# Who waits for the last store: the final semaphore wait of a row-mean kernel moved from SyncE to TensorE

## Chip, cores and metric

The kernel runs on one core of a Trainium2 chip. The time is device microseconds of that core; for the kernel before, three runs were taken and the median is given. Beside it there is one execution taken by the hardware profiler, with the records of its instructions, its semaphores and its DMA packets. The engines are called PE (TensorE), DVE (VectorE), ACT (ScalarE), POOL (GpSimd) and SP (SyncE), as in the profile.

## The reference

The input `x` is 32 x 512 x 1024 in float32 (67.1 MB). Each row of 1024 numbers is summed and divided by 1024:

```python
def reference(x, divisor):
    return (np.sum(x, axis=-1) / divisor).astype(np.float32)   # 32 x 512
```

## The kernel before

The 16384 rows are spread over the 128 partitions, 128 rows for each: 15 "first" rows, 97 "main" rows and 16 "last" rows per partition. SP issues every load and every store. Eight bulk loads (2 rows, then five of 16 rows, then two of 15 rows) go in turn through three large buffers, each with a semaphore of its own (`in_bulk0` to `in_bulk2`, numbers 99 to 101); a load waits until DVE, and ACT where it took rows, has finished with the buffer (lines L143 and L144). DVE sums whole rows with `reduce_sum` (L215). ACT takes a few rows of the last two bulk loads with an accumulating activation (L183). POOL scales the sums that are finished early (L157, L161). The last 16 rows of a partition come in four pieces of falling size; DVE's `both_halves` (L205) and ACT sum these into `fin`, already scaled. The order on each engine is written out by hand. PE computes nothing: its instructions are its share of the barriers among the engines at the start (recorded at L261 and L119), in which POOL raises semaphore 97 and the four others wake on it.

Three stores bring the result out, all issued by SP: `res0` at L148 (semaphore `out_first`, number 104), `res` at L150 (`out_main`, 105), and `fin` at L238, which waits until `done` (109) has reached 2 and adds 16 to `landed` (110) when it has landed. After that SP has three more steps. At L240 it waits for the first two stores (the second of these waits is carried by the instruction of L243), at L243 it clears the range of the kernel's other semaphores (99 to 109), and at L244 it waits until `landed` is 16 and takes 16 off again. `landed` is allocated after the others and lies outside the cleared range, so that the clearing need not wait for the last store.

Of the kernel before, what the change touches and what calls it, by code (L numbers as in the profile page):

```python
# [35 lines left out]
def kernel(  # L36
# [6 lines left out]
    nc = tc.nc  # L43
# [55 lines left out]
    landed = nc.alloc_semaphore("landed")  # L99
# [141 lines left out]
    ids = [s.num for s in sems.values()]  # L241
    assert max(ids) - min(ids) + 1 == len(ids)
    nc.sync.sem_clear(range(min(ids), max(ids) + 1))  # L243
    nc.sync.wait_ge(landed, 16).then_inc(landed, -16)  # L244


# [33 lines left out]
```

## Time and profile before

| what | value |
|---|---|
| median of 3 runs | 160.44 us (160.24 to 160.52) |
| span of the profiled execution, first to last instruction of the program | 159.3 us |
| DVE busy | 116.7 us (73%) |
| ACT busy | 18.6 us (12%) |
| POOL busy | 1.0 us (1%) |
| PE | no busy time; its last instruction is in the barrier at 1.8 us |
| DMA queue, share of 16 engines | 98.1%, 67.18 MB |
| last store (`fin`, 8.0 KB): issue, and issue to landing | 157.85 us, 1.4 us |

The span runs from the program's first instruction, the issue of the first load, to the end of its last, the wait of L244. What the device does before the first and after the last instruction of the program is in the time but not in the span; the two differ by 1.1 us here. The results give no time for the profiled execution itself, so its span is set beside the median of the three runs. The page counts waits, branches and DMA issues as no busy time; they are found as single records with a start and a duration in nanoseconds, in the answers for a source line. In those answers PE's sequencer stands as PEldq, SP's as SPq, and so on.

### The profile page before, as it was taken

Reading aid. Unit: us, or ns where it says so; the run is one execution under the profiler, and the core shown is the slowest. Engines: PE = TensorE matmul, PEld = TensorE weight load, DVE = VectorE, ACT = ScalarE, POOL = GpSimd, SP = SyncE. Lnnn points to the kernel's source line nnn. Section 1 sums busy time; section 2 is a strip of 40 time slices with the busy share of each in tenths; the row PEclk is TensorE's granted clock in tenths of the full one; section 3 lists DMA queues with packets and bytes.
Section 4 is the critical chain, followed back from the end, with each engine's and each line's share of the span. In section 5 each row is a group of like instructions: output and inputs, shape, how many; then the busy total and the mean of one; then the engine's idle time right before and its main releaser. Section 6 shows DMA issues by size and latency. Waiting matters only on the chain.

```text
span 159.3 us, 144 instructions
## 1 busy us (share of the span) xinstructions
DVE 116.7 (73%) x32; ACT 18.6 (12%) x35; POOL 1.0 (1%) x7
## 2 busy tenths in 40 slices
DVE  0500009999499994999949999499989990399296
ACT  3000000000000000000000000000009100392196
POOL 0000000000000000000000000000000001000000
DMA  8996996996996997979969969969996999889894
GB/s 296 494 527 263 527 527 263 527 527 263 527 527 263 527 444 346 527 313 477 527 263 527 527 263 527 494 278 463 494 494 262 478 494 494 350 350 525 344 401 154
DMA packets 2160, 67.18 MB, mean 422 GB/s; under 512 B 624, under 2 KB 752, under 8 KB 880
## 3 DMA queue, kind: packets, MB, share of 16 engines
q1 hardware_dynamic: 2160, 67.18, 98.1%
HBM read 67.11 MB, written 0.07 MB: 422 GB/s over the span
## 4 chain that ended last, share of the span: by engine, by line
DMA 67%; DVE 30%; another core or an unknown queue 1%; issue 0%
DMA bulk<-in_x_dram 67%; DVE res L215 29%; DVE bulk L205 1%; DVE tail L205 0%; DVE pb L205 0%; DVE fin L205 0%
## 5 line engine op out<-in xcount | busy, mean ns | idle before, releaser
L215 DVE TENSOR_REDUCE res<-bulk 128x16 f32<-128x16384 f32 (+3 forms) x8 | 110.0, 13754 | 37.7 <-DMA bulk<-in_x_dram 37.7
L183 ACT ACTIVATE junk<-bulk 128x1024 f32<-128x1024 f32 (+1 forms) x16 | 15.6, 973 | 137.2 <-DMA bulk<-in_x_dram 137.2
L205 DVE CUSTOM_DVE_ANT_0 bulk<-bulk 128x512 f32<-128x512 f32 (+1 forms) x9 | 5.5, 665 | 3.1 <-DMA bulk<-in_x_dram 3.1
L183 ACT ACTIVATION_READ_ACCUMULATOR junk<-bulk 128x1 f32 x16 | 3.0, 187 | 0.0
L183 ACT ACT_TABLE_LOAD x1 | 1.3, 1283 | 1.9 <-PEq L119 1.9
L157 POOL TENSOR_SCALAR res<-res 128x97 f32<-128x97 f32 x1 | 0.5, 465 | 129.8 <-DVE res L215 129.8
L205 DVE DVE_READ_ACCUMULATOR2_ANT fin<- 128x1 f32 x10 | 0.8, 82 | 0.0
L183 ACT ACTIVATE junk<-tail 128x737 f32<-128x737 f32 x1 | 0.8, 789 | 0.0
L205 DVE CUSTOM_DVE_ANT_0 bulk<-bulk,part 128x192 f32<-128x192 f32 x1 | 0.4, 420 | 0.3 <-DMA bulk<-in_x_dram 0.3
L205 DVE CUSTOM_DVE_ANT_0 tail<-tail 128x304 f32<-128x304 f32 x1 | 0.5, 476 | 0.0
L205 DVE CUSTOM_DVE_ANT_0 pb<-pb 128x209 f32<-128x209 f32 x1 | 0.4, 379 | 0.1
L161 POOL TENSOR_SCALAR res<-res 128x15 f32<-128x15 f32 x1 | 0.3, 262 | 15.6 <-DVE res L215 15.6
L183 ACT ACTIVATION_READ_ACCUMULATOR junk<-tail 128x1 f32 x1 | 0.2, 187 | 0.0
L153 POOL MEMSET pb<- 128x2 f32 x1 | 0.1, 99 | 1.5 <-POOLq L119 1.5
L261 POOL MEMSET const-bfloat16-1.0<- 128x1 bf16 x1 | 0.1, 101 | 0.0
L261 POOL MEMSET const-uint8-127<- 128x1 uint8 x1 | 0.1, 101 | 0.0
L261 POOL MEMSET const-float32-0.0<- 128x1 f32 x1 | 0.1, 98 | 0.2 <-issue 0.2
L261 POOL MEMSET const-float32-1.0<- 128x1 f32 x1 | 0.1, 98 | 0.0
L205 DVE DVE_READ_ACCUMULATOR2_ANT pb<- 128x1 f32 x1 | 0.1, 84 | 0.0
L205 DVE DVE_READ_ACCUMULATOR2_ANT part<- 128x1 f32 x1 | 0.1, 83 | 0.0
## 6 DMA issues: line engine op xcount, KB each, us to landing
bulk<-in_x_dram SPq DMA_DIRECT2D x2, 7680.0 KB, 39.3
bulk<-in_x_dram SPq DMA_DIRECT2D x1, 5440.0 KB, 32.0
bulk<-in_x_dram SPq DMA_DIRECT2D x1, 1872.0 KB, 23.5
bulk<-in_x_dram SPq DMA_DIRECT2D x1, 1024.0 KB, 4.6
tail<-in_x_dram SPq DMA_DIRECT2D x1, 672.0 KB, 24.7
pb<-in_x_dram SPq DMA_DIRECT2D x1, 208.0 KB, 24.8
bulk<-in_x_dram SPq DMA_DIRECT2D x5, 40.8
out_dram<-res SPq DMA_DIRECT2D x1, 48.5 KB, 1.6
```

Of the source, the lines that this page charges most:

```text
L153: nc.gpsimd.memset(pb[:, D - c15 :], 0.0).then_inc(pool)
L157: nc.gpsimd.tensor_scalar_mul(out=res, in0=res, scalar1=scale).then_inc(pool)
L161: nc.gpsimd.tensor_scalar_mul(out=res0, in0=res0, scalar1=scale).then_inc(pool)
L183: nc.scalar.activation(scratch, src, COPY, scale=by, accum_out=dst).then_inc(count)
L205: return nc.vector.tensor_tensor_reduce(out=src[:, :h], in0=src[:, :h], in1=src[:, h:], scale=by, scalar=ahead, op0=ADD, op1=ADD, accum_ou ...
L215: nc.vector.reduce_sum(out=dst[:, :m], in_=rows, axis=AX).then_inc(dve)
L261: nc = _bacc.Bacc("TRN2", target_bir_lowering=False, num_devices=1)
```

## The change

One line, the last of the kernel's body. The wait on `landed`, with the subtraction that goes with it, is issued on PE's queue where it was on SP's. In the built program the two kernels differ in the engine of this one instruction and in nothing else: all other instructions, their order on each engine, their semaphores and their waits are the same. SP's last instruction is then the clearing of L243; PE's last is the wait of L244, right behind its part of the starting barrier.

```diff
     ids = [s.num for s in sems.values()]
     assert max(ids) - min(ids) + 1 == len(ids)
     nc.sync.sem_clear(range(min(ids), max(ids) + 1))
-    nc.sync.wait_ge(landed, 16).then_inc(landed, -16)
+    nc.tensor.wait_ge(landed, 16).then_inc(landed, -16)
```

## The prediction

> **What bounds the kernel now.** I read the page first, for the engines and the chain; then the DMA answer for the last store; then the records of the two lines at which PE and SP do the same kind of step; last the semaphore records of the trace after the program's end.
>
> ```profile
> span 159.3 us, 144 instructions
> DVE 116.7 (73%) x32; ACT 18.6 (12%) x35; POOL 1.0 (1%) x7
> ...
> DMA 67%; DVE 30%; another core or an unknown queue 1%; issue 0%
> ```
>
> The span is loading and DVE's row sums. The change touches neither: no load, sum or store moves, so everything up to the landing of the last store stays where it is. PE has no busy time at all, so nothing of its own is delayed by a wait.
>
> ```profile
> out_dram<-fin SPq DMA_DIRECT2D x1, 8.0 KB, 1.4
> ```
>
> ```profile
> L244 SPq EVENT_SEMAPHORE  x1: 17/17/17, 159.3 to 159.3; - x1
> ```
>
> The last store is issued at 157.85 us and takes 1.4 us; its sixteenth increment is recorded at 159.259. SP's wait begins to execute at 159.275, 16 ns later, takes 17 ns, and the span ends at 159.292. This is the only instruction that changes its engine. What the same instruction costs on PE stands in the starting barrier, where all engines wake on one increment of POOL's:
>
> ```profile
> L119 SPq EVENT_SEMAPHORE  x2: 17/17/17, 1.5 to 1.8; - x2
> L119 ACTq EVENT_SEMAPHORE  x2: 17/17/17, 1.5 to 1.8; - x2
> L119 DVEq EVENT_SEMAPHORE  x2: 21/21/21, 1.5 to 1.8; - x2
> L119 PEldq EVENT_SEMAPHORE  x2: 51/51/51, 1.5 to 1.8; - x2
> ```
>
> PE's takes 51 ns where SP's takes 17. In the records, POOL's increments are at 1.159, 1.487 and 1.814; SP starts 16 ns after each, PE 28 or 29 ns after.
>
> So inside the span little can happen. The time, however, is 160.44 us and the span 159.29: 1.15 us lie around it. The semaphore records go on after the span, and there a semaphore that no line of the kernel touches, number 2, is raised in two runs of nine steps, with a sweep over nearly all other semaphore numbers between them. Times in us from the start of the span, as the records have them:
>
> ```
> semaphore 2, first pass:   2.129  157.924 157.963 158.007 159.437 159.480 159.518 159.553 159.599
> sweep, numbers 207..255 from 159.562, 156..206 from 159.632, 54..104 from 159.667,
>        105..155 from 159.670, 7..53 from 159.815 to 160.164
> semaphore 2, second pass: 160.388 160.423 160.461 160.504 160.528 160.626 160.664 160.698 160.745
> ```
>
> I read this as a check-in of the five engines in a fixed order, out (five records) and back (four). The first record is at 2.129, when only PE has ended its program (its last instruction ended at 1.894; ACT, DVE, POOL and SP had work to come): PE is first. The next comes 119 ns after ACT's last instruction ended at 157.805, and two more follow at 39 and 44 ns: ACT, POOL and DVE had finished. Then nothing until 159.437, 145 ns after SP's last instruction: SP is fifth, the turning point. Four steps back, at 159.599, the pass is over. The last sweep (7 to 53) begins only after that fourth step, it ends last, and the second pass begins 224 ns behind it: this is PE's. A third pass of nine, from -0.373 to -0.002, ends just before the first instruction and has the same steps.
>
> That order makes SP the cheapest engine to be late: four check-ins are already made while it waits, and only four steps (162 ns) follow it. PE is the dearest: the other four queue behind it, and the whole pass is still to run.
>
> **The change, part by part.** All from the landing at 159.259, which is common.
>
> 1. *Taken from SP.* 16 ns to wake, 17 ns to execute, 145 ns from there to SP's check-in (159.292 to 159.437), and 162 ns of return to the end of the pass: 340 ns. SP's last instruction is now the clearing of L243, recorded at 158.462 for 45 ns, so SP is ready some 0.75 us before the landing, and takes its place in the pass without delay.
>
> 2. *Given to PE: the wait.* 29 ns to wake and 51 ns to execute: 80 ns where SP had 33, so 47 ns more. The span shows this alone: 159.34 instead of 159.29. Bounds: SP's own 33 ns (no difference) and 80.
>
> 3. *Queued behind it on PE: its check-in.* Nothing else of the program stands behind PE's wait, but its check-in does, and ACT, POOL, DVE and SP wait in line for that. Before, it was over at 2.129, hidden behind 157 us. PE's step from the end of the same kind of instruction to its check-in is 1.894 to 2.129, 235 ns. Bounds: SP's 145 and PE's 235. I take 235: same engine and same step, and PE's gap from the end of its sweep to the second pass (224 ns) is as long. That is 90 ns more than SP's.
>
> 4. *The pass.* With PE late it runs whole. All four others are then waiting, as in the second pass, whose nine records take 357 ns (160.388 to 160.745); the one before the program took 371. Instead of 162, that is 195 ns more; 209 at the other bound.
>
> Sum: 80 + 235 + 357 = 672 ns after the landing instead of 340, so +0.332 us to the end of the first pass. PE's sweep starts behind the end of the pass as before and takes as long, so the rest moves by the same amount: 160.44 + 0.33 = 160.77. It is set against the median of three runs, because no separate time of the profiled execution is given; the trace supports that the closing is in the time, since from the span's end to the second pass is 1.10 us (159.292 to 160.388), against the 1.15 between span and median. Below, with SP's prices for points 2 and 3, the pass alone remains: +0.195. Above, with 371 for the pass: +0.346.
>
> [...]
>
> **The rivals.** The line at which a change counts is 0.2% of 160.44, 0.32 us, about what a measurement of this kernel can tell from no change. My sum lies just above it.
>
> *A: the full pass behind PE, as above.* 160.77, with its bounds 160.64 to 160.79 and the scatter of the runs (0.2 below and 0.08 above the median) around it.
>
> *B: the closing is not in the time.* If the time ends with the program's last instruction and the 1.15 us lie elsewhere (before the first instruction, say), point 2 alone remains: +0.047, 160.49. For it: the results do not say where the time ends. Against it: the closing fits the 1.15 us so closely.
>
> *C: PE is no slower than SP in these steps.* The 51 ns and 235 ns might belong to the program's start, when loads are being started beside them. Then PE's steps cost 33 and 145, and +0.195 is left: 160.64. Against it: PE is the slow one at the other end too, with 216 ns from the end of the pass to its sweep where SP's takes 125 (159.437 to 159.562). [...]
>
> *D, the other side: not slower.* The pass is not a fixed order but goes on from whoever is last. If the other four can check in while PE still waits and PE then turns at once into its sweep, PE no longer sits through the 162 ns of SP's return: it would pass at 159.259 + 80 + 235 = 159.574 instead of 159.599, a gain of 0.025 us, and at SP's prices 159.437, a gain of 0.162: 160.28 to 160.42. It decides if the records of number 2 show four check-ins before the landing. Against it: the pass before the program and the second one behind it have the same steps in the same order, and ACT, POOL and DVE checked in one after another within 83 ns though POOL had been idle since 148.2 us.
>
> *E: the change does not do what it says.* The build differs in the engine of that one instruction, and a wait for 16 on a semaphore that only the last store raises can't pass early; so 160.44, at little chance.
>
> **How the numbers follow.** A 0.74, B 0.09, C 0.07, D 0.08, E 0.02. Within A the nearest rows put the time above the line, and costs that I can't see from a PE that never waited this late add rather than subtract; I give 0.61 of its 0.74 to slower and 0.13 to within 0.2%. B, C and E are within. D by its own price is within; with a median of 160.24 it would read as faster, so half of it goes there. Slower 0.61, within 0.13 + 0.09 + 0.07 + 0.04 + 0.02 = 0.35, faster 0.04. The range goes from just below B, 160.45, to 161.00, A's upper bound of 160.79 with some 0.2 of scatter; D and E and the tail of A stay outside. A's own range is 160.64 to 161.00.
>
> **What would show it right or wrong.** In the profile of the changed kernel: L244 stands under PEldq, about 51 ns long and some 29 ns behind the last landing; the span is 0.05 us longer and all before it is unchanged. Semaphore 2 has no record near 2.1 us and none between there and the landing; nine records follow PE's end by 235 ns and take about 357; the sweep of 7 to 53 is 0.33 us later, counted from the landing. Four check-ins of number 2 ahead of the landing would show D; PE steps of 17 and 145 ns would show C; a closing that moves by 0.33 us with a time that does not would show B. A span that differs elsewhere by more than 0.1 us would mean that I have overlooked an effect before the landing.

## The result and the profile after

The changed kernel takes 160.74 us (median of 12 runs, 160.62 to 161.10) against 160.42 us (12 runs, 160.24 to 160.79) of the kernel before. The ratio is 1.0021, 95% interval 1.0014 to 1.0028: slower by 0.22 to 0.45 us.

The page of the changed kernel, in the lines that answer to those shown of before, hides this. Its span is even shorter:

```profile
span 159.0 us, 144 instructions
DVE 116.7 (73%) x32; ACT 18.7 (12%) x35; POOL 1.0 (1%) x7
...
DMA 67%; DVE 31%; another core or an unknown queue 1%; issue 0%
```

Where the two spans part can be found in the chain that ended last. It is the same, piece by piece and to 0.05 us, but for one stretch of loading (columns: start and length in us, what). Of the kernel before:

```profile
79.89 39.92 DMA bulk<-in_x_dram
119.81 0.02 issue
119.83 11.90 DVE res L215
```

Of the kernel after:

```profile
79.88 39.51 DMA bulk<-in_x_dram
119.39 0.02 issue
119.41 11.90 DVE res L215
```

The loads of that stretch, which the change doesn't touch, were 0.41 us quicker in this execution. The last store therefore landed at 158.900 us where it landed at 159.259. In the runs below, which have the same loads, the landing lies anywhere from 158.99 to 159.26. So the span of a single execution can't show an effect of this size; what follows the landing can. First, the answers for L244 and for the starting barrier:

```profile
L244 PEldq EVENT_SEMAPHORE  x1: 51/51/51, 158.9 to 158.9; - x1
```

```profile
L119 SPq EVENT_SEMAPHORE  x2: 17/17/17, 1.5 to 1.8; - x2
...
L119 PEldq EVENT_SEMAPHORE  x2: 51/51/51, 1.5 to 1.9; - x2
```

The wait now stands with PE's sequencer and takes the 51 ns of PE's other waits. The store itself landed as quickly as before:

```profile
out_dram<-fin SPq DMA_DIRECT2D x1, 8.0 KB, 1.4
```

Then the semaphore records behind the program, in us, of the changed kernel:

```
semaphore 2, first pass:  159.258 159.293 159.331 159.375 159.398 159.496 159.535 159.569 159.616
sweep 7..53:              159.833 to 160.180
semaphore 2, second pass: 160.404 160.438 160.477 160.521 160.544 160.643 160.681 160.715 160.762
```

No check-in comes near 2.1 us any more, and none before the landing. All nine follow PE's wait, with the steps that the second pass has, to 1 ns. From the landing, in ns ("wake" is the time from the store's last increment to the start of the wait's own record):

| | before (SP) | after (PE) | forecast for PE |
|---|---|---|---|
| wake | 16 | 28 | 29 |
| execute the wait | 17 | 51 | 51 |
| end of the wait to the check-in | 145 | 279 | 235 |
| from there to the end of the first pass | 162 | 358 | 357 |
| landing to end of first pass | 340 | 716 | 672 |
| landing to end of second pass | 1486 | 1862 | 1818 |

By these records the closing, from the landing to the end of the first pass, is 0.376 us longer. Of this, 0.196 us are the pass (358 ns instead of 162): four more steps on the way out take 140 ns, and the way back is 56 ns longer, because its first step, behind the fifth check-in, takes 98 ns where it took 43. The other 0.180 us are PE's own steps (12 ns more to wake, 34 to execute, 134 to check in). The time of this profiled execution is 160.64 us, 0.12 us less than the moment of its last check-in, 160.762.

### The profile page after: what moved, and what is told of

Same layout as the page of the kernel before. It is cut to its first block, busy times and chain, and to the rows that moved or that the text cites. A ratio compares the mean times of both kernels' runs of the same rounds, so it can differ in the third digit from the quotient of the medians.

```text
span 159.0 us, 144 instructions
## 1 busy us (share of the span) xinstructions
DVE 116.7 (73%) x32; ACT 18.7 (12%) x35; POOL 1.0 (1%) x7
## 4 chain that ended last, share of the span: by engine, by line
DMA 67%; DVE 31%; another core or an unknown queue 1%; issue 0%
DMA bulk<-in_x_dram 67%; DVE res L215 29%; DVE bulk L205 1%; DVE pb L205 0%; DVE tail L205 0%; DVE fin L205 0%
```

## The experiments

All edits are against the kernel before; the diffs show the lines that matter and leave out where an added semaphore is allocated. "Closing" is the stretch from the last store's landing to the ninth check-in of the first pass; it is 340 ns before and 716 ns after the change.

**The wait on ScalarE**

```diff
-    nc.sync.wait_ge(landed, 16).then_inc(landed, -16)
+    nc.scalar.wait_ge(landed, 16).then_inc(landed, -16)
```

Expected:

> The wait for the last store on ScalarE, otherwise the kernel before. Theory (a fixed order PE, ACT, POOL, DVE, SP and back; whoever waits holds up all behind it): ACT wakes in about 20 ns, executes in 17, checks in 119 (ACT's row of before) to 145 ns (SP's) later, and then eight steps less the first one are left: 358 - 35 = 323 ns. From the landing to the end of the first pass 480 to 505 ns against 340 before: 0.14 to 0.17 us slower than before, 0.2 us faster than with PE. In the semaphore records one check-in (PE's) near 2.1 us, the other eight behind the landing. Rival (it is PE that is slow, the order is nothing): ACT executes in 17 ns as SP does, so within 0.05 us of before, with three or four check-ins ahead of the landing.

Measured: ratio 1.0009 (1.0001 to 1.0018), that is 0.02 to 0.29 us slower. In its answer for L244:

```profile
L244 ACTq EVENT_SEMAPHORE  x1: 17/17/17, 159.0 to 159.0; - x1
```

ACT's wait costs the 17 ns that SP's costs, and yet the kernel is slower. One check-in, at 2.128, is ahead of the landing (159.016), eight are behind it, from 159.204 to 159.526. Wake 21, execute 17, check-in 150 and rest of the pass 322 ns make a closing of 510 ns, 0.17 us more than before. The order of the pass costs time: the rest of the pass is 322 ns here and 162 with SP, and ACT's own steps account for 10 ns of the difference.

**The wait on GpSimd**

```diff
-    nc.sync.wait_ge(landed, 16).then_inc(landed, -16)
+    nc.gpsimd.wait_ge(landed, 16).then_inc(landed, -16)
```

Expected:

> The wait for the last store on GpSimd, otherwise the kernel before. Theory of the fixed order: PE and ACT have checked in before the landing, seven records follow it. POOL wakes in 16 to 21 ns, executes in 17, checks in some 145 ns later, and 358 - 73 = 285 ns of the pass are left: about 465 ns against 340, 0.12 us slower than before. Rival (PE alone is slow): within 0.05 us of before.

Measured: ratio 1.0035 (1.0021 to 1.0048), 0.34 to 0.77 us slower, the dearest of all. The expectation, 0.12 us, was wrong in size. Two check-ins (2.146 and 157.720) are ahead of the landing and seven behind, and the pass still needs 285 ns, both as the order says. But POOL's step from the wait to its check-in is 562 ns, not 145:

```profile
L244 POOLq EVENT_SEMAPHORE  x1: 17/17/17, 159.2 to 159.2; - x1
```

The wait ends at 159.168, POOL's check-in stands at 159.730. The closing is 887 ns, 0.55 us more than before, which the time bears out.

**The wait on VectorE**

```diff
-    nc.sync.wait_ge(landed, 16).then_inc(landed, -16)
+    nc.vector.wait_ge(landed, 16).then_inc(landed, -16)
```

Expected:

> The wait for the last store on VectorE, otherwise the kernel before. Theory of the fixed order: PE, ACT and POOL have checked in before the landing, six records follow it. DVE wakes in 28 ns, executes in 21, checks in 145 to 184 ns later, and 358 - 117 = 241 ns of the pass are left: 435 to 475 ns against 340, 0.10 to 0.13 us slower than before. Rival (PE alone is slow): within 0.05 us of before.

Measured: ratio 1.0005 (0.9996 to 1.0015); the time alone leaves it open whether it is slower.

```profile
L244 DVEq EVENT_SEMAPHORE  x1: 21/21/21, 159.3 to 159.3; - x1
```

The records don't leave it open: three check-ins ahead of the landing, six behind, wake 28, execute 21, check-in 188, rest of the pass 241 ns, a closing of 478 ns, 0.14 us more than before. The check-ins of the first pass in the three runs, in us; those ahead of the landing stand to the left of it:

```
ACT waits:   2.128 | landing 159.016 | 159.204 159.242 159.286 159.309 159.406 159.446 159.480 159.526
POOL waits:  2.146 157.720 | landing 159.128 | 159.730 159.774 159.797 159.895 159.934 159.968 160.015
DVE waits:   2.127 157.884 157.922 | landing 159.261 | 159.498 159.521 159.619 159.658 159.692 159.739
```

Together with the kernels before and after, the three runs place the engines: with ACT waiting one check-in is early, with POOL two, with DVE three, with SP four, with PE none. The four records behind SP's they do not place: that these are the way back through the other engines is the prediction's reading.

**PE waits late, but not last**

```diff
-    for s in (out_main, out_first):
-        nc.sync.wait_ge(s, 16)
+    nc.tensor.wait_ge(out_main, 16).then_inc(by_pe)
+    for s, n in ((out_first, 16), (by_pe, 1)):
+        nc.sync.wait_ge(s, n)
```

Expected:

> The wait for the last store stays on SyncE. TensorE waits for the store of res (out_main, landed near 158.45 us) in SyncE's place and tells SyncE by one more semaphore before the clearing. Theory: PE is done near 158.55 and checks in 235 to 279 ns later, ACT, POOL and DVE by 158.95, all ahead of the last landing; SyncE's chain behind the landing is untouched at 340 ns: the same time as before within 0.05 us, though PE's wait ends late in the program. It also shows whether PE's step to its check-in is 235 ns (as at the start of before) or 279 ns (as after) behind a late wait that no DMA's last landing is waiting on. Rival (any wait that parks PE to the end is dear): slower by some 0.3 us, as the change is.

Measured: ratio 1.0002 (0.9994 to 1.0010). PE's wait is there, with its 51 ns, late in the program:

```profile
L239 PEldq EVENT_SEMAPHORE  x1: 51/51/51, 158.3 to 158.3; - x1
```

It ends at 158.317, and the check-ins of PE, ACT, POOL and DVE follow at 158.596, 158.630, 158.668 and 158.713, all before the landing at 159.116. SP's is at 159.296, and the closing is 345 ns. Here a slow wait on PE, over before the last landing, costs nothing that the time can show (the interval is 0.1 us below to 0.16 us above no change). Its step to the check-in is 279 ns here too, so the longer step isn't due to being last.

**GpSimd waits late, but not last**

```diff
+    nc.gpsimd.wait_ge(out_main, 16).then_inc(by_pool_late)
```

with SP waiting on `by_pool_late` before the clearing, as in the run above. Expected:

> GpSimd waits for the store of res (out_main, landed near 158.25 us) in SyncE's place and tells SyncE before the clearing; the last wait stays on SyncE. With GpSimd as the last waiter the step from its wait to its check-in was 562 ns, where 145 were expected. If that is a step of GpSimd's own: again about 560 ns, so its check-in comes near 158.85, DVE's by 158.90, both ahead of SyncE's near 159.3, and the time is that of before within 0.05 us. If GpSimd's step was long only because it was last: about 145 ns, the same time. Rival to the fixed order (a dear engine costs wherever it waits): 0.2 to 0.5 us slower than before.

Measured: ratio 0.9996 (0.9987 to 1.0006). POOL's wait ends at 158.307 and its check-in is at 158.868, a step of 561 ns: it belongs to POOL, whether POOL is last or not.

```profile
L239 POOLq EVENT_SEMAPHORE  x1: 17/17/17, 158.3 to 158.3; - x1
```

The check-in lies ahead of the landing (159.117), the closing is 340 ns, and the 561 ns cost nothing that the time can show.

**Why PE's step to the check-in was 279 ns and not 235.** Six kernels give PE early waits. In five of them SP keeps the last wait; in the third, PE has it too. The first has this edit:

```diff
+    nc.tensor.wait_ge(in_bulk[0], 16).then_inc(by_pe)
...
+    nc.sync.wait_ge(by_pe, 1)
```

> What is tested is the one term that came out larger than forecast: from the end of TensorE's wait to its check-in, 279 ns in the changed kernel and in the run with TensorE's wait for the store of res, 235 ns in the kernel before. Here the last wait stays on SyncE, and TensorE waits for the first load (landed near 4.58 us, some 2.7 us of waiting) and tells SyncE by a semaphore that is awaited before the clearing. If a wait of some length adds the 44 ns: 279 ns. If each instruction of the body behind the barrier adds 44 ns, whatever its wait: 279 ns. If it is the lateness in the program (over 100 us): 235 ns. The time is that of before within its scatter in every case, as TensorE checks in near 5 us.

Measured: 274 ns. That leaves the length of the wait or its place among PE's instructions, not lateness.

> The same with TensorE waiting for GpSimd's small memset (by_pool, near 2.02 us), about 0.1 us of waiting. If a wait of some length adds the 44 ns: 235 ns from its end to the check-in. If each instruction behind the barrier adds 44 ns: 279 ns. If lateness: 235 ns. Time as before.

Here the wait is `nc.tensor.wait_ge(pool, 1)`. Measured: 274 ns although the wait ends at 2.116, so neither lateness nor length.

> TensorE waits for the first load, as in the run of the early long wait, and then for the last store, as in the change. If a wait of some length or lateness adds the 44 ns: 279 ns from the end of the second wait to the check-in. If each instruction behind the barrier adds 44 ns: 323 ns. The time is that of the changed kernel, 0.3 us above before, or 0.35 us in the second case; from the last landing to the end of the second pass 1.86 us (1.91 us) against 1.49 us before.

Measured: 275 ns, so no 44 ns for each instruction either; none of the three ideas (length, lateness, 44 ns for each instruction) fits all three runs. The kernel itself repeats the result of the change: ratio 1.0021 (1.0011 to 1.0031), a closing of 711 ns and 1857 ns from the landing to the end of the second pass.

> TensorE waits four times for the first load, an early event, and the last wait stays on SyncE. The step from the end of TensorE's last wait to its check-in was 235 ns with no instruction of the body behind the barrier, 274 to 279 ns with one, and 275 ns with two. If any instruction of the body moves it to one new value: 274 to 279 ns again. If it goes by where the stream ends (9 instructions gave the short step; 13 would lie as 9 does in blocks of four): 235 ns. Time as before.

Measured: 234 ns.

```profile
L238 PEldq EVENT_SEMAPHORE  x4: 51/51/51, 4.9 to 5.4; - x4
```

The records of PE's four waits show a longer gap among themselves; each takes 51 ns, and they start at 4.935, 5.086, 5.281 and 5.432 us. Between the end of one and the start of the next are 100, 144 and 100 ns.

> TensorE waits three times for the first load, so its stream has 12 instructions; the last wait stays on SyncE. In the run with four waits the gaps between them were 100, 144 and 100 ns, and the step to the check-in was 234 ns. If 44 ns belong to one place in every four instructions of TensorE's stream (there between the second and the third wait): gaps of 100 and 144 ns here, and 235 ns to the check-in. If four waits or more make the step short: 275 ns. Time as before.

> TensorE waits five times for the first load, 14 instructions in its stream; the last wait stays on SyncE. If 44 ns belong to one place in every four instructions: gaps of 100, 144, 100 and 100 ns, and the next such place lies in the step to the check-in, 279 ns. If four waits or more make the step short: 235 ns. Time as before.

Measured: with three waits gaps of 100 and 144 ns and 235 ns to the check-in; with five waits gaps of 100, 144, 100 and 100 ns and 234 ns. The five kernels whose last wait stays on SP took 160.35 to 160.56 us, one run each, which is within the scatter of the kernel before, and their closings are 340 to 343 ns. All six fit one reading: the 44 ns lie at one place of PE's stream (its instructions in order), behind the second instruction of the body. With three or more instructions PE has passed it by then, with one or two it falls into the step to the check-in, and with none, as before the change, the step would end short of it. That the place returns every four instructions, the first of the two ideas for the run with five, is refuted. What the sequencer does there stays open, as do the 4 to 5 ns between 274 or 275 and 279, and whether such a place would come again further on was not tried.

## Why the prediction was right

- **The step that decided it, the order of the pass, held in each run.** The number of early check-ins with PE, ACT, POOL, DVE and SP as last waiter was 0, 1, 2, 3 and 4, and the rest of the pass from the waiter's own check-in took 358, 322, 285, 241 and 162 ns. Behind PE's wait it runs whole, in single steps of 23 to 98 ns: 196 ns more than before (358 less 162), where the sum had 195.
- **The closing is in the time.** Rival B falls: in the twelve profiled executions that have a time of their own, the time is 0.11 to 0.13 us less than the moment of the last check-in, while it exceeds the span by between 1.3 and 1.9 us according to who waits (160.49 against 159.149 with PE's early wait, 161.04 against 159.168 with POOL's). For the kernel before no time of the profiled execution is given. By that offset it would be about 160.62 us, an estimate above its median; its landing was one of the two latest. The runs listed with a time and a span say the same without those records: time less span (spans are given to 0.1 us, so means alone serve) is 1.65 us in the mean of the twelve runs after the change and 1.32 to 1.34 in three groups of 12 to 29 runs of the kernel before (1.49 with ACT, 1.45 with DVE, 1.89 with POOL waiting). That what the device does ahead of the first instruction is in the time too, as said beside the profile of before, is not shown.
- **One argument for it held by luck.** The prediction set 1.10 us, from the span's end to the start of the second pass, beside 1.15 between span and median. But the span came from an execution that landed late and the median from other runs; time less span is about 1.33 us within one run, and by the offset above the time, counted from the first instruction, would end inside the second pass, about 0.12 us ahead of its last check-in. The close fit was chance, though what it was taken to show is so.
- **Wake and execution of PE's wait**: 28 and 51 ns, against 29 and 51 in the sum.
- **PE's check-in, point 3, was mis-sized.** The row of before gave 235 ns as the upper bound; it was 279. The row was PE's own and of the same kind, but by the reading above the place in the stream with the 44 ns lay just behind it. The sum by the records is +0.376 us instead of +0.332. The median moved by 0.32 us with an interval of 0.22 to 0.45; it can't tell the two apart, nor does it by itself prove more than the 0.2%, since its lower end lies below 0.32. That the median came out just above that line and not just below it is partly luck. Time less span can tell the sums apart: in the means it grew by 0.31 to 0.34 us, and with the 0.05 by which PE's wait lengthens the span that is 0.36 to 0.38, the sum by the records and not 0.332.
- **Rival C falls**: PE's steps are 51 and 279 ns late in the program as well, not 17 and 145. The other argument against it, that PE's sweep starts later behind the pass than SP's (216 ns against 125), rested on my reading of the order: no record here names the engine of a sweep.
- **Rival D falls** with the run on PE itself: no engine checks in ahead of PE. GpSimd's early wait shows the same in small: DVE, idle since 157.674, checks in only 44 ns after POOL's 158.868.
- **What I gave as a sign of error did occur and was none.** The span differed by more than 0.1 us ahead of the landing (0.36). One stretch of loads was quicker in that execution. Spans scatter as widely without any change: from 159.0 to 159.6 us in 29 runs of the kernel before on one chip, and from 159.0 to 159.4 in the twelve runs after the change. The limit was too narrow for this kernel, and counting from the landing is the right way to compare.

No experiment pointed to a kernel that beats the one before. The last waiter with the shortest closing is SP (340 ns; DVE, the next, has 478), which had the wait already.

## What to carry to other kernels

In every profile here the landing of the last store is followed by a closing of 340 to 887 ns, in which the last waiter and the engines behind it in the order check in one after another, and the time includes it: time less span is 1.32 to 1.34 us in the mean with SP waiting last, 1.65 with PE and 1.89 with POOL. Give the last wait to the engine with the shortest closing. Here that is SP (340 to 345 ns), which checks in as the last of the five and has the shortest step from its wait to its check-in (143 to 147 ns; ACT, the next, has 150). The place in the order alone does not decide it: POOL comes behind PE and ACT, and with its 562 ns it was still the dearest, with the closing of 887 ns. Let the other engines finish ahead of the last landing; the two runs with late waits of PE and GpSimd show no cost of them there (ratios 1.0002 and 0.9996). Look behind the span: where time and span differ by more in one kernel than in another, look for the difference in the records after the last instruction, as here. When an effect is below a microsecond, measure it from the nearest common event (here the landing of the last store), not from the start.

## What was not expected of the hardware

- From the end of its last wait to its check-in GpSimd takes 561 and 562 ns, where SP takes 143 to 147, ACT 150, DVE 188 and PE 234 to 279. The cause was not looked into.
- In the closing, the first step of the way back, from the fifth check-in (SP's) to the sixth, takes 97 or 98 ns in the runs where SP stands waiting for its turn, and 43 or 44 where SP is the last to come. The sum of the prediction had this in its 357 ns, since it was read from a pass in which all wait. The cause is open.
- PE's sequencer takes 51 ns for a wait where SP, ACT and POOL take 17 and DVE 21, and in the runs with three to five early waits 100 ns pass from the end of one to the start of the next; at one place in its stream that gap is 144 ns.
- Loads that are the same in each kernel let the last store land anywhere between 158.90 and 159.26 us in thirteen profiles.
